# Retention scores in alternating halves, and two thirds of the feed-forward transposes by VectorE and DMA, in a two-block transformer

## The chip, the cores and the metric

The kernel runs on one core of one Trainium2 chip. The metric is the device time of one execution in microseconds (us).

## What is computed

Two blocks, one after the other, on a sequence of 256 rows of width 1024. The first block has two layers: retention with memory attention, a feed-forward, differential attention with memory attention, a feed-forward. The second has one layer: a state-space mixer beside a forgetting attention, and a feed-forward whose 5632 columns go through a causal convolution of three taps along the sequence. What the change touches is this:

```python
# retention, per head (dk 64): scores, decayed by distance
s_in = jnp.einsum('bnihd,bnjhd->bnhij', q, k) * d_in
# first block, both layers (FFN_DIM 2816)
gu = h @ w_gate_up[layer]
x = x + (jax.nn.silu(gu[..., :FFN_DIM]) * gu[..., FFN_DIM:]) @ w_down[layer]
# second block (D_FF 2816, three taps)
h = causal_depthwise_conv(x @ w_up, conv_w, conv_b)
gate, val = jnp.split(h, 2, axis=-1)
x = x + (jax.nn.silu(gate) * val) @ w_down
```

## The kernel before

All large products are computed in three matmuls of a rounded type: each operand is a high part and a low part, and high x high, high x low and low x high are summed in PSUM. Weights come by DMA in units of 256 rows by up to 512 columns (512 KB) into a ring of four staging buffers (`st`); ACT casts a unit to its high part (`wh`), DVE subtracts to get the low part (`wl`), each in a ring of six buffers. Activations stand with the sequence (256 rows, two tiles `t` of 128) in the partitions after a projection, and have to be turned before they can be the left operand of the next product: TensorE transposes blocks of 128x128 into PSUM, and ACT and DVE split the result into `lth` and `ltl` (ring of ten).

**Feed-forward.** `ffn` walks over six chunks of columns, five of 512 and one of 256. For a chunk, `act` runs a gate projection and a value (up) projection, each eight steps of the inner dimension by two `t` by three matmuls: 48 slots. The order is act(0), act(1), down(0), act(2), down(1), act(3) and so on, where down(n) adds the product of chunk n with `w_down` (four units, which all stay in their buffers until both `t` are done) into four PSUM banks of the pool `psa`, which has five. So what turns a chunk has one down section and the next chunk's two projections in which to finish, and for chunk 0 the projections alone.

In `ffn1` (first and second feed-forward) ACT writes the activated gate to `sg`, DVE multiplies it with the value projection, and a task per `t` transposes four blocks and splits them (lines 777 to 787). In `ffn2` (third) ACT copies each projection to `uu`; `conv_tiles` (line 823) transposes half a chunk at a time into one bank, in the order channel block by `t`, so that a channel's 256 positions stand in one partition; `conv` computes the taps out of PSUM into `cc`; then gate and value are multiplied and split.

**Retention.** `pair_task` in `mixer0` (line 974) computes for two heads, which lie in partitions 0 to 63 and 64 to 127 of `qkT`, the scores of both sequence tiles in one PSUM bank per head: two matmuls for the first head, its multiplication with the decay on DVE, then the same for the second.

**Order.** The program is written by a planner (`Weave`) that keeps an estimated clock per engine. Side work is a task (a generator) that says when it can go on; `poll` is called between the matmuls and emits the steps whose planned time has come, and `fill` emits weight DMAs, casts and subtractions when buffers come free. Every engine then runs its instructions in the order in which they were emitted. All DMAs are issued from the queue of SyncE (SP), line 257. All operations go through one helper and carry line 89.

Of the kernel before, what the change touches and what calls it, by code (L numbers as in the profile page):

```python
# [7 lines left out]
F32 = mybir.dt.float32  # L8
# [214 lines left out]
def _build(tc, a, out, stop):  # L223
# [6 lines left out]

    cp, wp, lp, nrm, sm = pool("cp"), pool("wp"), pool("lp"), pool("nrm"), pool("sm")
    ps_pools = pool("psm", space=PSUM), pool("psa", space=PSUM)


    def ring(p, n, tag, bufs, dtype=F32):
# [29 lines left out]

    W.clock["Q"] = 500.0

    def rsqrt(ss, n, inv):

        v, y = small([P, n], "r"), small([P, n], "r")  # L270
        G.tensor_scalar(v, ss, inv, EPS, op0=ALU.mult, op1=ALU.add)
        G.tensor_tensor(y, v, mhalf[:, :n], op=ALU.pow)
        return y
# [16 lines left out]
    def transposes(ps, srcs):  # L290
        for i, s_ in enumerate(srcs):
            T.transpose(ps[:, i * P : (i + 1) * P], s_, ident)

    def blocks(t_, n=4):
        return [t_[:, b * P : (b + 1) * P] for b in range(n)]
# [471 lines left out]
    def ffn1(l, H, nxt):  # L767
        with tc.tile_pool(name=W.name("ff"), bufs=1) as fp:
            w = a["w_gate_up"][l]
            sgr = ring(fp, 512, "sg", 6)  # L770

            def act(c0, nn, serial):
                sg = [sgr.get(True) for _ in range(2)]
                proj(w, H, c0, nn, lambda t, ps, r: S.activation(sg[t][:, :nn], ps[:, :nn], AF.Silu, scale=r), serial)
                got = [None, None]

                def task(t):
                    yield psa, 1
                    ps = psa.get(True)
                    transposes(ps, blocks(sg[t], nn // P))  # L780
                    sgr.close(sg[t])
                    yield
                    lt = yield from lt_tiles()
                    yield from split(lt[0][:, :nn], lt[1][:, :nn], ps[:, :nn])
                    psa.close(ps)
                    yield
                    return lt

                def ev(t, ps, r):
                    V.scalar_tensor_tensor(sg[t][:, :nn], ps[:, :nn], r, sg[t][:, :nn], op0=ALU.mult, op1=ALU.mult)  # L790
                    got[t] = go(task(t), W.clock["V"])

                proj(w, H, FF + c0, nn, ev)

                def both():
                    yield got
                    lts = [g.val for g in got]
                    return lambda k, t: tuple(z[:, (k * P - c0) : (k * P - c0) + P] for z in lts[t]), lts

                return go(both())  # L800

            return ffn(a["w_down"][l], H, nxt, act)
# [11 lines left out]
    def ffn2(H, nxt):  # L814
        with tc.tile_pool(name="ff2", bufs=1) as fp:
            w = a["w_up_2"]
            uur, ccr = ring(fp, 512, "uu", 6), ring(fp, 512, "cc", 6)

            def tiles(c0, nn, serial):
                us = [uur.get(True) for _ in range(2)]  # L820
                return us, proj(w, H, c0, nn, lambda t, ps, r: S.activation(us[t][:, :nn], ps[:, :nn], AF.Copy, scale=r), serial)

            def conv_tiles(us, c0, q):
                yield psa, 1
                ps = psa.get(True)
                transposes(ps, [us[t][:, (2 * q + b) * P : (2 * q + b + 1) * P] for b in range(2) for t in range(2)])
                yield ccr, 1
                res = ccr.get(True)
                ch = c0 // P + 2 * q
                yield from conv(ps, [res[:, b * 256 : (b + 1) * 256] for b in range(2)], C_FW + 3 * ch, C_FB + ch, 3)  # L830
                psa.close(ps)
                yield
                return res

            def act(c0, nn, serial):
                ug, got_g = tiles(c0, nn, serial)

                def gate():
                    yield [got_g]
                    gts = []  # L840
                    for q in range(nn // 256):
                        gt = yield from conv_tiles(ug, c0, q)
                        gts.append(gt)
                    uur.close(*ug)
                    for gt in gts:
                        S.activation(gt[:], gt[:], AF.Silu)
                    yield
                    return gts

                gt_ = go(gate())  # L850
                uv, got_v = tiles(FF + c0, nn, False)

                def task():
                    yield [got_v, gt_]
                    lts = []
                    for q in range(nn // 256):
                        gt = gt_.val[q]
                        vt = yield from conv_tiles(uv, FF + c0, q)
                        V.tensor_tensor(gt[:], gt[:], vt[:], op=ALU.mult)
                        ccr.close(vt)  # L860
                        yield
                        lt = yield from lt_tiles()
                        yield from split(lt[0][:], lt[1][:], gt[:])
                        ccr.close(gt)
                        lts.append(lt)
                    uur.close(*uv)
                    yield

                    def lhs(k, t):
                        i = k - c0 // P  # L870
                        o = (i % 2) * 256 + t * P
                        return tuple(z[:, o : o + P] for z in lts[i // 2])

                    return lhs, lts

                return go(task())

            return ffn(a["w_down_2"], H, nxt, act)
# [51 lines left out]
    def mixer0(H, nxt, first):  # L930
# [43 lines left out]
        def pair_task(pair, deps):  # L974
            yield deps
            sTs = []
            for hh in range(2):
                yield psa, 1
                r0 = 64 * hh
                st = psa.get(True)  # L980
                T.matmul(st[:, 0:256], qkT[r0 : r0 + 64, 3 + pair, 0:P], qkT[r0 : r0 + 64, pair, :], start=True, stop=True)
                T.matmul(st[:, 256:384], qkT[r0 : r0 + 64, 3 + pair, P : 2 * P], qkT[r0 : r0 + 64, pair, P : 2 * P],
                         start=True, stop=True)
                yield sTr, 1
                sT = sTr.get(True)
                V.tensor_tensor(sT[:], st[:, :384], dtab[:, 2 * pair + hh, :], op=ALU.mult)
                psa.close(st)
                sTs.append(sT)
            yield psa, 1
            ob = psa.get(True)  # L990
            for hh in range(2):
                sT = sTs[hh]
                v = [blk(768 + (2 * pair + hh) * P, t) for t in range(2)]
                T.matmul(ob[:, hh * P : (hh + 1) * P], sT[:, 0:P], v[0], start=True, stop=True)
                o1 = ob[:, 256 + hh * P : 256 + (hh + 1) * P]
                T.matmul(o1, sT[:, P : 2 * P], v[0], start=True, stop=False)
                T.matmul(o1, sT[:, 2 * P : 3 * P], v[1], start=False, stop=True)
                sTr.close(sT)
            yield
            on = onr.get(True)  # L1000
            yield from head_norm(ob, hsq, on)
            c, r = divmod(1536 + pair * 256, 512)
            while c not in E:
                yield 500
            yield [E[c]]
            for t in range(2):
                V.tensor_tensor(on[:, t * 256 : (t + 1) * 256], on[:, t * 256 : (t + 1) * 256],
                                u[c, t][:, r : r + 256], op=ALU.mult)
            yield psa, 1
            ps = psa.get(True)  # L1010
            transposes(ps, blocks(on))
            onr.close(on)
            yield
            lt = yield from lt_tiles()
# [796 lines left out]
```

## Time and profile before

| | us |
|---|---|
| median of 3 runs | 1037.08 (1036.85 to 1037.44) |
| the profiled execution | 1037.33 |
| its span, first to last instruction | 1035.4 |
| TensorE busy | 1027.5 |
| VectorE busy | 672.8 |
| ScalarE busy | 603.8 |

Busy times and rows are of the one profiled execution. Matmuls overlap in the pipeline, so a row's duration is longer than the slot between two starts; what a TensorE instruction costs is read from starts. The three feed-forwards lie at about 136 to 321, 428 to 614 and 842 to 1036 us.

### The profile page before, as it was taken

The numbers are of one execution on the slowest core, as the hardware profiler recorded it, in microseconds if no ns is written. First come the engines' busy times: TensorE is split into PE (matmuls) and PEld (weight loads), VectorE is DVE, ScalarE is ACT, GpSimd is POOL, SyncE is SP. The second block draws the span as 40 slices with busy tenths as digits, with TensorE's granted clock in tenths as the row PEclk, the third lists the DMA queues.
The fourth block names the chain that finished last, engine by engine and source line by source line (L and its number), as shares of the span: only waits on it lengthen the run. The fifth ranks groups of instructions, "written<-read, shape, count | busy, mean of one in ns | idle before, by whom it ended". The sixth has DMA issues, their size and how long they took to land.

```text
span 1035.4 us, 14058 instructions
## 1 busy us (share of the span) xinstructions
PE 1027.5 (99%) x5177; PEld 856.5 (83%) x5177; DVE 672.8 (65%) x1013; ACT 603.8 (58%) x974; POOL 68.1 (7%) x93
## 2 busy tenths in 40 slices
PE   9999999999999999999999999999999999999998
PEld 7878888888898778888888988888888888888887
DVE  5665575554556887755454467878888577767755
ACT  7647564444445886644444446686776566656553
POOL 1121000000001231100000001100300010000000
PEclk9999999999999999999999999999999999999999
DMA  7763555655565433565565457515523655566533
GB/s 248 261 203 127 163 185 181 192 182 155 182 203 171 142 122 124 182 210 190 151 204 192 150 151 220 186 41 179 167 82 99 193 161 178 171 196 204 177 116 114
DMA packets 98822, 174.93 MB, mean 169 GB/s; under 512 B 6976, under 2 KB 22080, under 8 KB 98624
## 3 DMA queue, kind: packets, MB, share of 16 engines
q1 hardware_dynamic: 98752, 174.02, 53.3%
q8 instruction: 41, 0.67, 0.3%
q14 instruction: 29, 0.24, 0.1%
HBM read 172.95 MB, written 1.05 MB: 168 GB/s over the span
## 4 chain that ended last, share of the span: by engine, by line
PE 92%; ACT 2%; DVE 2%; DMA 2%; POOL 1%; issue 1%; SPq 0%; ACTq 0%
PE psm L89 59%; PE psa L89 33%; DMA st<-w_in 1%; POOL s8r L89 1%; DMA xt<-x 1%; ACT wh L89 1%; ACT pd L89 0%; DVE wl L89 0%; POOL s16r L89 0%; DVE s L89 0%; SPq L257 0%; DVE pd L89 0%; ACT qkT L89 0%; POOL s4r L89 0%; DVE s16g L89 0%
## 5 line engine op out<-in xcount | busy, mean ns | idle before, releaser
L89 DVE TENSOR_TENSOR wl<-st,wh 128x1024 fp32r<-128x1024 f32 (+2 forms) x339 | 389.9, 1169 | 212.3 <-ACT wh L89 211.4
L89 ACT CAST wh<-st 128x1024 fp32r<-128x1024 f32 (+2 forms) x339 | 334.8, 1007 | 228.0 <-PE psm L89 100.5
L89 PE MATMUL psm<-wh,lth 128*128 128x512 f32 (+2 forms) x1024 | 395.8, 387 | 0.0
L89 PE MATMUL psm<-wl,lth 128*128 128x512 f32 (+2 forms) x1024 | 385.8, 377 | 0.0
L89 PE MATMUL psm<-wh,ltl 128*128 128x512 f32 (+2 forms) x1024 | 381.1, 377 | 0.1
L89 PEld LDWEIGHTS psm<-wh,ltl 128*128 128x128 f32 x1024 | 192.6, 188 | 36.8 <-DVE ltl L89 0.8
L89 PEld LDWEIGHTS psm<-wh,lth 128*128 128x128 f32 x1024 | 192.9, 188 | 33.7 <-issue 1.2
L89 PEld LDWEIGHTS psm<-wl,lth 128*128 128x128 f32 x1024 | 193.0, 188 | 32.9 <-DVE wl L89 1.0
L89 PE MATMUL psa<-wh,lth 128*128 128x512 f32 x328 | 132.2, 403 | 0.0
L89 PE MATMUL psa<-wl,lth 128*128 128x512 f32 x328 | 128.0, 390 | 0.0
L89 PE MATMUL psa<-wh,ltl 128*128 128x512 f32 x328 | 105.1, 390 | 0.0
L89 PEld LDWEIGHTS psa<-wh,ltl 128*128 128x128 f32 x328 | 61.6, 188 | 13.2
L89 PEld LDWEIGHTS psa<-wh,lth 128*128 128x128 f32 x328 | 61.7, 188 | 11.2
L89 PEld LDWEIGHTS psa<-wl,lth 128*128 128x128 f32 x328 | 61.7, 188 | 11.2
L89 DVE SCALAR_TENSOR_TENSOR cc<-psa,ccol,cc 128x255 f32<-128x255 f32 (+1 forms) x88 | 36.3, 476 | 18.5 <-ACT cc L89 18.3
L89 POOL TENSOR_SCALAR s1n<-s1n 128x1 f32<-128x1 f32 x14 | 5.1, 368 | 469.6 <-ACT sq L89 469.5
L89 DVE SCALAR_TENSOR_TENSOR sg<-psm,s1n,sg 128x512 f32<-128x512 f32 (+1 forms) x24 | 17.0, 707 | 20.6 <-PE psm L89 20.5
L89 ACT ACTIVATE cc<-psa,ccol 128x256 f32<-128x256 f32 x44 | 22.4, 560 | 12.9 <-PE psa L89 12.6
L89 ACT CAST lth<-psa 128x512 fp32r<-128x512 f32 (+1 forms) x30 | 16.6, 555 | 22.4 <-PE psa L89 22.3
L89 ACT ACTIVATE sq<-xt 128x512 f32<-128x512 f32 x24 | 15.3, 636 | 21.5 <-DVE xt L89 20.9
L89 DVE TENSOR_TENSOR ltl<-psa,lth 128x512 fp32r<-128x512 f32 (+1 forms) x30 | 19.6, 653 | 12.7 <-ACT lth L89 12.7
L89 ACT ACTIVATE sg<-psm,s1n 128x512 f32<-128x512 f32 (+1 forms) x24 | 15.7, 653 | 14.4 <-PE psm L89 14.4
(210 smaller groups left out, 856.3 us busy)
## 6 DMA issues: line engine op xcount, KB each, us to landing
st<-w_gate_up SPq DMA_DIRECT2D x80, 512.0 KB, 4.3
st<-w_in SPq DMA_DIRECT2D x67, 512.0 KB, 4.3
st<-w_down SPq DMA_DIRECT2D x66, 512.0 KB, 4.7
st<-w_up SPq DMA_DIRECT2D x40, 512.0 KB, 3.8
st<-w_out SPq DMA_DIRECT2D x32, 512.0 KB, 3.8
st<-w_in SPq DMA_DIRECT2D x30, 256.0 KB, 3.9
st<-w_mem_kv SPq DMA_DIRECT2D x8, 512.0 KB, 4.9
st<-w_gate_up SPq DMA_DIRECT2D x16, 256.0 KB, 2.8
```

The source lines that it names most:

```text
L89: f(*args, **kw)
```

## The change

A helper `flip` turns two tiles of 128x512 without TensorE. DVE transposes every square of 32x32 (two instructions into `sq32`, 128x1024); four DMAs write the result to a buffer in memory, one for each quarter of the partitions, in runs of 128 elements (512 B); one DMA reads the buffer back into `fl` (128x1024), in which the columns of a block lie in the order of an interleave. `unmix` and `mixed` are access patterns that undo it. All five DMAs are issued by SP.

In `ffn1` chunks whose first column is below 2048 (four of six) use it for both `t` together, and the splits read `fl`. In `ffn2` the same chunks use it once for the gate and once for the value; an ACT copy (`na`) puts the result in the order that `conv_tiles` takes, and the convolution reads `na` in SBUF in place of a PSUM bank. In `pair_task` two banks are taken at once, and the four score matmuls alternate between the heads.

```diff
+    scr = Ring(W, pool("scr", space=bass.MemoryType.DRAM), [2 * P, 512], F32, "scr", 4)
...
+    def flip(srcs, sqs, dst):
+        yield sqs, 1
+        sq = sqs.get(True)
+        for t, src in enumerate(srcs):
+            V.transpose(sq[:, t * 512 : (t + 1) * 512].rearrange("p (s b j) -> p s b j", s=4, b=4),
+                        src.rearrange("p (b s j) -> p s b j", b=4, s=4))
+        yield
+        m = scr.get(True)
+        m4 = m[:].rearrange("(t s i) (q n) -> q i (t s) n", t=2, s=4, q=4)
+        yield 300 + move(m[:], sq[:], [(m4[q], sq[32 * q : 32 * q + 32, :].rearrange("p (u n) -> p u n", u=8)) for q in range(4)])
+        sqs.close(sq)
+        yield 300 + move(dst[:], m[:], [(dst[:].rearrange("p (t n) -> p t n", t=2), m[:].rearrange("(t p) n -> p t n", t=2))])
+        scr.close(m)
...
+            sgr, sqs, flr = ring(fp, 512, "sg", 6), ring(fp, 1024, "sq32", 2), ring(fp, 1024, "fl", 2)
...
+                    yield from flip([z[:] for z in sg], sqs, fl)
+                    sgr.close(*sg)
+                    for t in range(2):
+                        lt = yield from lt_tiles()
+                        yield from split(mixed(lt[0][:]), mixed(lt[1][:]), unmix(fl, t))
...
-                    got[t] = go(task(t), W.clock["V"])
+                    if c0 >= 2048:
+                        got[t] = go(task(t), W.clock["V"])
+                    elif t == 1:
+                        got[:] = [go(flips(), W.clock["V"])]
...
+            def turned(us):
+                yield flr, 1
+                fl = flr.get(True)
+                yield from flip([z[:] for z in us], sqs, fl)
+                uur.close(*us)
+                yield nar, 1
+                na = nar.get(True)
+                S.copy(na[:].rearrange("p b (m j) -> p b m j", m=8), fl[:].rearrange("p (m b j) -> p b m j", m=8, b=4))
...
-                yield from conv(ps, [res[:, b * 256 : (b + 1) * 256] for b in range(2)], C_FW + 3 * ch, C_FB + ch, 3)
+                yield from conv(src, [res[:, b * 256 : (b + 1) * 256] for b in range(2)], C_FW + 3 * ch, C_FB + ch, 3)
...
-            for hh in range(2):
-                yield psa, 1
-                r0 = 64 * hh
-                st = psa.get(True)
-                T.matmul(st[:, 0:256], qkT[r0 : r0 + 64, 3 + pair, 0:P], qkT[r0 : r0 + 64, pair, :], start=True, stop=True)
-                T.matmul(st[:, 256:384], qkT[r0 : r0 + 64, 3 + pair, P : 2 * P], qkT[r0 : r0 + 64, pair, P : 2 * P],
-                         start=True, stop=True)
+            yield psa, 2
+            sts = [psa.get(True), psa.get(True)]
+            for b, cols in ((0, slice(0, 256)), (1, slice(256, 384))):
+                for hh, st in enumerate(sts):
+                    rows = slice(64 * hh, 64 * hh + 64)
+                    T.matmul(st[:, cols], qkT[rows, 3 + pair, b * P : (b + 1) * P], qkT[rows, pair, b * P :],
+                             start=True, stop=True)
+            for hh, st in enumerate(sts):
                 yield sTr, 1
```

## Rows read from the trace of the kernel before

**Rows 1.** The page, part 1: busy us, share of span, instructions.
```profile
PE 1027.5 (99%) x5177; PEld 856.5 (83%) x5177; DVE 672.8 (65%) x1013; ACT 603.8 (58%) x974; POOL 68.1 (7%) x93
```
**Rows 2.** Chain of waits in time, first feed-forward: start us, us, what.
```profile
191.03 21.76 PE psm L89 x96
212.79 11.80 PE psa L89 x56
```
**Rows 3.** Stretches, one chunk each: us, busy per engine, clock, DMA share, GB/s.
```profile
212.79:246.35 33.56, 33.56 (x155) 27.81 (x153) 17.14 (x16) 14.77 (x16) 0.00 (x0) 1.00 0.62 187
921.70:956.17 34.47, 34.47 (x161) 28.57 (x161) 23.23 (x32) 20.68 (x29) 0.00 (x0) 1.00 0.61 184
```
**Rows 4.** Groups by form, TensorE: transposes; busy, mean ns, idle before.
```profile
L89 PE MATMUL psa<-pcol,sg 128*128 128x128 f32 x88 | 13.5, 271 | 0.0
L89 PE MATMUL psa<-pcol,uu 128*128 128x128 f32 x88 | 13.2, 272 | 0.0
```
**Rows 5.** TensorE in order of time: four transposes in the first feed-forward.
```profile
178.84 0.39 PE L89 MATMUL psm<-wh,ltl 128*128 128x512 f32 x1
179.07 0.60 PE L89 MATMUL psa<-pcol,sg 128*128 128x128 f32 x4
...
179.98 0.39 PE L89 MATMUL psa<-wh,lth 128*128 128x512 f32 x1
```
**Rows 6.** TensorE in order of time, mixer0: one head's scores, then two.
```profile
36.39 0.39 PE L89 MATMUL psm<-wh,ltl 128*128 128x512 f32 x1
36.71 0.92 PE L89 MATMUL psa<-qkT 64*128 64x256 f32 x4
...
38.12 0.40 PE L89 MATMUL psm<-wh,ltl 128*128 128x512 f32 x1
...
49.76 0.39 PE L89 MATMUL psm<-wh,ltl 128*128 128x512 f32 x1
50.08 1.57 PE L89 MATMUL psa<-qkT 64*128 64x256 f32 x8
...
52.15 0.40 PE L89 MATMUL psm<-wh,ltl 128*128 128x512 f32 x1
```
**Rows 7.** TensorE in order of time, mixer1: two halves' scores, alternating.
```profile
346.34 0.39 PE L89 MATMUL psm<-wh,ltl 128*128 128x512 f32 x1
346.66 0.93 PE L89 MATMUL psa<-qkT 64*128 64x128 f32 x8
...
348.08 0.39 PE L89 MATMUL psm<-wh,ltl 128*128 128x512 f32 x1
```
**Rows 8.** Groups by form, ACT and DVE.
```profile
L89 ACT CAST wh<-st 128x1024 fp32r<-128x1024 f32 x305 | 314.4, 1050 | 196.0 <-PE psm L89 88.9 <-PE psa L89 54.6 <-DMA st<-w_down 12.2
L89 ACT CAST lth<-psa 128x512 fp32r<-128x512 f32 x26 | 15.2, 583 | 22.3 <-PE psa L89 22.3
L89 ACT CAST lth<-cc 128x512 fp32r<-128x512 f32 x11 | 6.8, 619 | 15.0 <-DVE cc L89 14.9
L89 DVE TENSOR_TENSOR ltl<-psa,lth 128x512 fp32r<-128x512 f32 x26 | 17.9, 689 | 11.9 <-ACT lth L89 11.9
```
**Rows 9.** Instructions on tile st, SP's issues: ns min/median/max, first and last start.
```profile
L257 SPq DMA_DIRECT2D st<-w_gate_up x96: 367/368/702, 108.6 to 583.4; - x96
```
**Rows 10.** SP's waits, third feed-forward: us in total, times, longest.
```profile
SPq L257 <- DVE wl L89: 128.7, 57, 8.7
```
**Rows 11.** Stretch of a down section, instructions on st alone: DVE, ACT, clock, DMA.
```profile
921.70:933.50 11.80, 2.44 (x2) 3.33 (x4) 1.00 0.41 131
```
**Rows 12.** DMA issues: count, KB each, median us to landing.
```profile
st<-w_gate_up SPq DMA_DIRECT2D x80, 512.0 KB, 4.3
out<-xt SPq DMA_DIRECT2D x4, 256.0 KB, 2.2
```
**Rows 13.** TensorE in order of time, third feed-forward: a value's two half tiles.
```profile
864.82 0.60 PE L89 MATMUL psa<-pcol,uu 128*128 128x128 f32 x4
...
872.08 0.60 PE L89 MATMUL psa<-pcol,uu 128*128 128x128 f32 x4
```

More of the change, by code (lines that the diff above doesn't have):

```diff
@@ L266, in _build, with move @@
     W.clock["Q"] = 500.0
+    def move(dst, src, parts):
+        for d, s_ in parts:
+            nc.sync.dma_start(d, s_)
+        k, n = dst.tensor.name, src.size() if callable(src.size) else src.size
+        W.clock["Q"] = max(W.clock["Q"], W.now, W.done.get(src.tensor.name, 0.0)) + 480 * len(parts)
+        W.clock["D"] = max(W.clock["D"], W.clock["Q"] + 1100) + n * 4 / 360.0
+        W.done[k] = W.used[k] = W.clock["D"] + 900
+        W.used[src.tensor.name] = W.clock["D"]
+        W.by[k] = "D"
+        return W.done[k] - W.now
     def rsqrt(ss, n, inv):
@@ L292, in transposes, with unmix, mixed @@
             T.transpose(ps[:, i * P : (i + 1) * P], s_, ident)
+    def flip(srcs, sqs, dst):
[11 more added lines that the diff above has]
+        scr.close(m)
+    def unmix(dst, t):
+        return dst[:, t * 512 : (t + 1) * 512].rearrange("p (q b j) -> p b q j", q=4, b=4)
+    def mixed(ap):
+        return ap.rearrange("p (b q j) -> p b q j", q=4, b=4)
     def blocks(t_, n=4):
@@ L769, in ffn1 @@
             w = a["w_gate_up"][l]
-            sgr = ring(fp, 512, "sg", 6)
+            sgr, sqs, flr = ring(fp, 512, "sg", 6), ring(fp, 1024, "sq32", 2), ring(fp, 1024, "fl", 2)
             def act(c0, nn, serial):
@@ L787, in task, with flips @@
                     return lt
+                def flips():
+                    yield flr, 1
+                    fl = flr.get(True)
+                    yield from flip([z[:] for z in sg], sqs, fl)
+                    sgr.close(*sg)
+                    lts = []
+                    for t in range(2):
+                        lt = yield from lt_tiles()
+                        yield from split(mixed(lt[0][:]), mixed(lt[1][:]), unmix(fl, t))
+                        lts.append(lt)
+                    flr.close(fl)
+                    yield
+                    return lts
                 def ev(t, ps, r):
                     V.scalar_tensor_tensor(sg[t][:, :nn], ps[:, :nn], r, sg[t][:, :nn], op0=ALU.mult, op1=ALU.mult)
-                    got[t] = go(task(t), W.clock["V"])
+                    if c0 >= 2048:
+                        got[t] = go(task(t), W.clock["V"])
+                    elif t == 1:
+                        got[:] = [go(flips(), W.clock["V"])]
                 proj(w, H, FF + c0, nn, ev)
@@ L796, in both @@
                     yield got
-                    lts = [g.val for g in got]
+                    lts = got[0].val if len(got) == 1 else [g.val for g in got]
                     return lambda k, t: tuple(z[:, (k * P - c0) : (k * P - c0) + P] for z in lts[t]), lts
@@ L817, in ffn2 @@
             uur, ccr = ring(fp, 512, "uu", 6), ring(fp, 512, "cc", 6)
+            sqs, flr, nar = ring(fp, 1024, "sq32", 2), ring(fp, 1024, "fl", 2), ring(fp, (4, 256), "na", 2)
             def tiles(c0, nn, serial):
@@ L821, in tiles, with conv_tiles @@
                 return us, proj(w, H, c0, nn, lambda t, ps, r: S.activation(us[t][:, :nn], ps[:, :nn], AF.Copy, scale=r), serial)
-            def conv_tiles(us, c0, q):
-                yield psa, 1
-                ps = psa.get(True)
-                transposes(ps, [us[t][:, (2 * q + b) * P : (2 * q + b + 1) * P] for b in range(2) for t in range(2)])
+            def turned(us):
+                yield flr, 1
+                fl = flr.get(True)
+                yield from flip([z[:] for z in us], sqs, fl)
[3 more added lines that the diff above has]
+                S.copy(na[:].rearrange("p b (m j) -> p b m j", m=8), fl[:].rearrange("p (m b j) -> p b m j", m=8, b=4))
+                flr.close(fl)
+                yield
+                return na
+            def conv_tiles(us, c0, q, na):
+                if na is None:
+                    yield psa, 1
+                    ps = psa.get(True)
+                    transposes(ps, [us[t][:, (2 * q + b) * P : (2 * q + b + 1) * P] for b in range(2) for t in range(2)])
+                src = ps[:] if na is None else na[:, 2 * q : 2 * q + 2, :].rearrange("p b n -> p (b n)")
                 yield ccr, 1
@@ L829, in conv_tiles @@
                 ch = c0 // P + 2 * q
-                yield from conv(ps, [res[:, b * 256 : (b + 1) * 256] for b in range(2)], C_FW + 3 * ch, C_FB + ch, 3)
-                psa.close(ps)
+                yield from conv(src, [res[:, b * 256 : (b + 1) * 256] for b in range(2)], C_FW + 3 * ch, C_FB + ch, 3)
+                if na is None:
+                    psa.close(ps)
+                elif 2 * q + 2 == 4:
+                    nar.close(na)
                 yield
@@ L840, in gate @@
                     gts = []
+                    na = (yield from turned(ug)) if c0 < 2048 else None
                     for q in range(nn // 256):
-                        gt = yield from conv_tiles(ug, c0, q)
+                        gt = yield from conv_tiles(ug, c0, q, na)
                         gts.append(gt)
-                    uur.close(*ug)
+                    if na is None:
+                        uur.close(*ug)
                     for gt in gts:
@@ L853, in task @@
                 def task():
-                    yield [got_v, gt_]
+                    yield [got_v]
+                    na = (yield from turned(uv)) if c0 < 2048 else None
+                    yield [gt_]
                     lts = []
@@ L857, in task @@
                         gt = gt_.val[q]
-                        vt = yield from conv_tiles(uv, FF + c0, q)
+                        vt = yield from conv_tiles(uv, FF + c0, q, na)
                         V.tensor_tensor(gt[:], gt[:], vt[:], op=ALU.mult)
@@ L865, in task @@
                         lts.append(lt)
-                    uur.close(*uv)
+                    if na is None:
+                        uur.close(*uv)
                     yield
@@ L976, in pair_task @@
             sTs = []
-            for hh in range(2):
-                yield psa, 1
-                r0 = 64 * hh
-                st = psa.get(True)
-                T.matmul(st[:, 0:256], qkT[r0 : r0 + 64, 3 + pair, 0:P], qkT[r0 : r0 + 64, pair, :], start=True, stop=True)
-                T.matmul(st[:, 256:384], qkT[r0 : r0 + 64, 3 + pair, P : 2 * P], qkT[r0 : r0 + 64, pair, P : 2 * P],
-                         start=True, stop=True)
+            yield psa, 2
[6 more added lines that the diff above has]
+            for hh, st in enumerate(sts):
                 yield sTr, 1
```

## Prediction

> **What bounds the kernel now.** The page's busy times come first: TensorE (PE) is busy for 1027.5 of 1035.4 us, VectorE (DVE) for 672.8, ScalarE (ACT) for 603.8 [rows 1]. A full PE row says little by itself, so the second view is the chain of waits in order of time. Inside the feed-forwards it is nothing but PE: 96 matmuls in 21.76 us for the two projections of a chunk, then 56 instructions in 11.80 us for a down section [rows 2]. So a matmul of 512 columns has a slot of 21.76/96 = 0.2267 us, and no wait lies between them. An edit there is worth the PE slots that it removes, as long as weights and left operands still arrive in time. The third view is the table of stretches: in a steady chunk of the first feed-forward DVE works 17.1 of 33.6 us, ACT 14.8 and the DMA engines 62%; in the third DVE works 23.2 of 34.5, ACT 20.7, DMA 61% [rows 3].
>
> **Transposes removed.** A chunk below column 2048 (four of six) loses its TensorE transposes: two groups of four in each of the first two feed-forwards, four groups in the third. That is 64 of the 88 of sg and 64 of the 88 of uu [rows 4], 32 groups in all. One group: from the matmul before it (178.84) to the third matmul after it (179.98) [rows 5] are 1.14 us, where three slots take 0.68; it costs 0.46. The chain says the same: 11.80 less 48 slots of 0.2267 (10.88) is 0.92 for two groups [rows 2]. The gain is 32 x 0.46 = **14.7 us**, all of it on the path.
>
> **Scores in turns.** Retention's score matmuls use 64 rows of the array. Now two of a head stand together, then two of the other head on the other rows. Such a group of four records takes 38.12 - 36.39 = 1.73 us less 0.68 of ordinary slots, 1.05; where both heads stood in one row (eight records, head after head) 52.15 - 49.76 - 0.68 = 1.71 [rows 6]. Mixer1's heads hold the same shapes, already alternated between the halves: eight records in 348.08 - 346.34 - 0.68 = 1.06 [rows 7]. Before there are four single groups and one double one: 4 x 1.05 + 1.71 = 5.9; after, three alternated: 3.2. The gain is **2.7 us**, and nothing if the halves don't overlap here; I take 2.7, since rows 7 are the same shapes. The first wait for two free banks instead of one; the waiting is the program's planner's, behind which matmuls of the projections go on, and I cost it at nothing (if two banks are late, PE loses up to one group, 1 us).
>
> **What is added.** There are 16 round trips: four in each of the first two feed-forwards, eight in the third. Each has two DVE transposes of 128x512, four DMAs of 128 KB into memory in rows of 512 B (1024 packets), and one of 512 KB back. DVE: no row shows its square transpose; the ops of that size, 689 ns [rows 8], are the nearest, and twice that is the other end, for the four-way access pattern. In the third feed-forward a chunk has four: 23.2 + 4 x 0.69 = 26 us, at most 28.7, of the 32.6 us that a chunk has left (34.47 less 1.83). DVE becomes the bound only from 2.4 us for one. ACT gets a copy of 1024 columns per round trip in the third alone, 1.05 us like a weight cast [rows 8]: 20.7 + 2.1 of 32.6. Reading the conversions' sources from SBUF instead of PSUM I take at about the same price: a cast of 512 columns takes 583 ns from PSUM and 619 from SBUF [rows 8]. All of it lies beside PE.
>
> SP: a weight DMA costs its queue 0.37 us [rows 9], so five cost 1.8 us per round trip. In order on that queue the read-back waits until the write has landed, and weight loads stand behind it. They can wait: SP already waits for DVE to free staging, 128.7 us of the third feed-forward [rows 10], so loads run ahead with four staged units. Converted weights run ahead less: six buffers, of which a down section holds four, so two units of 2.72 us (12 matmuls), 5.4 us of cover. In such a section DVE converts only two, 2.44 us [rows 11].
>
> DMA engines: a chunk's 12 units of 256 packets take 0.62 x 33.56 us x 16 engines / 3072 = 108 ns for one packet of 2 KB. A packet of 512 B costs between a quarter of it (27 ns) and the whole (108), so the writes of a round trip take 1.7 to 6.9 us and the read 1.7. The first two feed-forwards reach at most 20.8 + 8.6 = 29.4 of 32.6 us, covered. The third has 21.0 + 6.9 = 28 at the low end and 38 at the high one. I take a value near the low end (bytes, not packets, as the load of 4.3 us for 512 KB beside 2.2 us for a 256 KB store suggests [rows 12]); the high end is a rival.
> The Trainium skill, page "DMA: Bandwidth & Descriptors", section Specifications, gives 512 B as the smallest transfer at line rate; by it the write costs the low end, an estimate of 1.7 us, and the sum stays as it is. No row here shows such a store.
>
> **The new wait.** After a projection ends: evacuation 0.7 us, transposes 1.4, one weight conversion ahead of them 1.2 [rows 11], four issues 1.5 [rows 9], landing 2.2 to 4.3 (I take 4), read-back 0.4 + 4.3 [rows 12], for a total of 13.5. The first two feed-forwards add a multiplication (0.7) and four splitting ops (some 2.7): 17 us. The third adds the copy with its queue (2): 15.5, then the convolution of one half tile, which today is paced 872.08 - 864.82 = 7.3 us [rows 13], some 6 without TensorE: halves at 21.5 and 27.5 us. These are wanted after the next chunk's projections and one down section (32.6 us), so they are in time, except for chunk 0, which has no down section between: 21.8 us and, for the second half, 24.5. That makes no wait in the first two feed-forwards and about **3 us** in the third (bounds 0 and 6).
>
> **Sum.** 1037.33 (this execution's own time; span 1035.4) - 14.7 - 2.7 + 3.0 = 1022.9. The median of the runs is 0.25 lower: **1022.7**.
>
> **Rivals.** (1) As forecast, 1019.5 to 1026: 62%. (2) The scores gain nothing: 1025.4, 8%. For it, the second group could sit where PE then waits for DVE; against it, rows 7. (3) Round trips land late everywhere: ACT and DVE are in order, so a copy that waits for the read-back holds up weight casts behind it. If both landings double, ACT stands 8 us instead of being covered for 5.4, and PE loses 2.6 us at perhaps four of the 16, 10 us: 1033, 16%, spread over 1026 to 1035. (4) **Slower:** packets bind, not bytes. In the third feed-forward a chunk has 21.0 + 2 x (1.7 + 64 p) us of DMA, with p the packet's time. From p = 64 ns DMA outlasts PE; from 98 ns four chunks give back all 17.4; at 108 ns each is 38.3 long, 5.6 over, 22.6 in all: 1037.3 - 17.4 + 22.6 = 1042.5. 9%: against it speaks that every other store and load here scales with its bytes. (5) The store is slower by an order, since its strides do part of the transposing: if each row of 512 B cost four packets of 108 ns, it would take 27.6 us and a round trip 29.3. The first feed-forwards' chunks would be 50.1 us long and the third's 79.6, 8 x 17.5 + 4 x 47.0 = 328 us: 1348, 2%. Against it, the innermost step of the copy is one element, and DVE has turned the squares before it.
> The Trainium skill, page "VectorE: DVE Perf Modes", section "The three transpose paths", warns of this: a plain copy whose strides do the transposing is 19 times slower than the transposing DMA when the innermost destination stride is large, and its rules give full 128x128 blocks to TensorE. By that factor on 1.7 us, an estimate of 32 us, the time would be near that of (5). (6) Effects cancel within 0.2% (2.1 us, what a measurement of this kernel can tell from no change): 3%.
> Together: faster 0.86, same 0.03, slower 0.11. The range takes (1), (2) and most of (3), with planner noise of 1 us below: 1018.8 to 1031.
>
> **What would show it.** Right: no sg transposes by TensorE but 24, chunks of 32.65 us in all three feed-forwards, a PE gap of some 3 us ahead of the third's first down section and none elsewhere; eight-record score groups of 0.85 us in mixer0; DVE transposes near 0.69 us. Wrong: PE waiting for wl or wh in the chunks (3), DMA share at 0.9 and more with loads landing far above 4.3 us (4, 5), a granted clock below 1.00 after the gap.

## The result and the profile after

The changed kernel takes 1019.81 us in the median (1019.48 to 1021.1, four runs); the kernel before, run beside it, 1037.26 (1036.85 to 1037.97, four runs). The ratio is 0.9833, 95% interval 0.9819 to 0.9847. The forecast was 1022.7: right in direction, the time inside the range and 2.9 us shorter than forecast. The profiled execution took 1019.89, with a span of 1018.1 us, 17.3 less than that of [rows 1]. One execution of a variant below took 3612 us, and its time and trace are left out.

The page of the changed kernel: busy us, share of the span, instructions; below it the two kinds of DMA of a round trip (count, KB each, median us to landing).

```profile
PE 1008.9 (99%) x5049; PEld 842.0 (83%) x5049; DVE 691.0 (68%) x1045; ACT 611.6 (60%) x982; POOL 67.8 (7%) x93
...
scr<-sq SPq DMA_DIRECT2D x64, 128.0 KB, 4.5
fl<-scr SPq DMA_DIRECT2D x16, 512.0 KB, 5.1
```

TensorE executes 128 instructions fewer, which are the 32 groups of four transposes, and is still busy 99% of the span: what was taken off its queue shortened the span. The chain of waits of the changed kernel shows the same chunk as [rows 2], then the third feed-forward (start us, us, what):

```profile
186.62 21.76 PE psm L89 x96
208.38 10.88 PE psa L89 x48
...
877.93 7.82 PE psa L89 x33
885.75 21.76 PE psm L89 x96
907.50 10.88 PE psa L89 x48
```

A down section of 11.80 us has become 10.88 us, its 48 matmuls and nothing else, in the first feed-forward and in the third. The stretches (columns as in [rows 3]): a steady chunk of the third, one of the first, and then the projections of the third's chunk 1, which alone cover the turning of chunk 0's value:

```profile
907.50:940.14 32.64, 32.64 (x146) 27.03 (x145) 25.76 (x37) 22.65 (x30) 0.00 (x0) 1.00 0.77 240
219.26:251.90 32.64, 32.64 (x145) 27.04 (x145) 18.24 (x19) 14.63 (x17) 0.00 (x0) 1.00 0.71 226
851.91:873.67 21.76, 21.76 (x97) 18.02 (x96) 17.77 (x29) 18.24 (x25) 0.00 (x0) 1.00 0.83 270
```

Both steady chunks last 32.64 us, where [rows 3] had 33.56 and 34.47. DVE is busy for 79% of the first row, 56% of the second and 82% of the third (17.77 of 21.76). Some 4 us behind that last stretch stands the only new wait of TensorE in a feed-forward. TensorE, VectorE and one row of ACT, in order of time:

```profile
877.93 0.50 PE L89 MATMUL psa<-wl,lth 128*128 128x512 f32 x1 [0.70 <-DVE wl L89]
```
```profile
874.08 1.30 DVE L89 STREAM_TRANSPOSE sq<-uu 128x512 f32<-128x512 f32 x2
876.05 0.69 DVE L89 TENSOR_TENSOR ltl<-cc,lth 128x512 fp32r<-128x512 f32 x1 [0.66 <-ACT lth L89]
876.65 3.49 DVE L89 TENSOR_TENSOR wl<-st,wh 128x1024 fp32r<-128x1024 f32 x3
```
```profile
874.46 1.04 ACT L89 CAST wh<-st 128x1024 fp32r<-128x1024 f32 x1
```

The low part of a `w_down` unit stood on VectorE behind `ltl`, and `ltl` waited 0.66 us for ACT, whose conversion `lth` began only at 875.40, behind a weight cast (874.46). The two squares of the next gate (874.08) had ended by then, so they didn't make this wait. PE stood 0.70 us. By starts, the down section takes 885.75 - 873.67 = 12.08 us instead of 10.88: the wait costs 1.2 us in all. By stage, the span's difference of 17.3 us is: mixer0 3.1 gained, the first feed-forward 3.7, the second 3.7, mixer2 0.7, the third feed-forward 6.3, the end behind TensorE's last instruction 0.3, less a start that was 0.5 later in this execution.

### The profile page after: what moved, and what is told of

It reads as the page before. It is cut to its first block, busy times and chain, and to the rows that moved or that the text cites. A ratio compares the mean times of both kernels' runs of the same rounds, so it can differ in the third digit from the quotient of the medians.

```text
span 1018.1 us, 13938 instructions
## 1 busy us (share of the span) xinstructions
PE 1008.9 (99%) x5049; PEld 842.0 (83%) x5049; DVE 691.0 (68%) x1045; ACT 611.6 (60%) x982; POOL 67.8 (7%) x93
## 4 chain that ended last, share of the span: by engine, by line
PE 93%; DVE 2%; ACT 2%; POOL 1%; DMA 1%; issue 1%; SPq 0%; ACTq 0%
PE psm L89 61%; PE psa L89 32%; POOL s8r L89 1%; DVE wl L89 0%; ACT pd L89 0%; DMA st<-w_in 0%; DMA fl<-scr 0%; DVE ltl L89 0%; ACT wh L89 0%; POOL s16r L89 0%; DVE s L89 0%; ACT lth L89 0%; DVE pd L89 0%; ACT qkT L89 0%; POOL s4r L89 0%
## 5 line engine op out<-in xcount | busy, mean ns | idle before, releaser
L89 DVE SCALAR_TENSOR_TENSOR cc<-na,ccol,cc 128x255 f32<-128x255 f32 (+1 forms) x64 | 27.2, 480 | 6.1 <-ACT cc L89 6.0
L89 ACT ACTIVATE uu<-psm,s1n 128x512 f32<-128x512 f32 (+1 forms) x24 | 15.6, 651 | 15.7 <-PE psm L89 15.6
L89 POOL TENSOR_TENSOR s16r<-s16r,mhalf 128x16 f32<-128x16 f32 x7 | 22.2, 3178 | 0.6
```

The source lines that it names most:

```text
L89: f(*args, **kw)
```

## Experiments

**The scores alone.** The kernel before with the diff of `pair_task` only:

```diff
-            for hh in range(2):
-                yield psa, 1
+            yield psa, 2
+            sts = [psa.get(True), psa.get(True)]
+            for b, cols in ((0, slice(0, 256)), (1, slice(256, 384))):
+                for hh, st in enumerate(sts):
```

> Only the score matmuls alternate; all feed-forward transposes stay on TensorE. Theory (the halves of the array overlap, and TensorE is the path in mixer0): 2.7 us less by the prediction's groups, 3.1 if pairs 1 and 2 stand together in one row as in the changed kernel, so a ratio of 0.9970 to 0.9974. Rival (the freed slots are filled by a later wait, such as that for the memory keys): no change, 1.000.

Measured: 1034.38 us (5 runs) against 1038.0, ratio 0.9964 (0.9951 to 0.9978). The stretch of mixer0 that holds all score groups, from the same matmul to the same matmul, in the kernel before and then in this one:

```profile
22.70:74.42 51.72, 51.20 (x253) 41.54 (x253) 35.32 (x45) 28.21 (x42) 10.96 (x14) 1.00 0.70 231
```
```profile
24.47:73.07 48.60, 48.08 (x253) 39.87 (x253) 35.09 (x45) 27.93 (x42) 10.72 (x14) 1.00 0.75 246
```

The same 253 instructions take 51.72 - 48.60 = 3.1 us less: the part is worth the same without the rest of the change. Another 0.5 of the 3.6 us lies in mixer2, which no part of the change touches (its account stands further below).

**The first two feed-forwards alone.** Scores and third feed-forward as before: in `ffn2` no chunk is turned by squares.

```diff
-                    na = (yield from turned(ug)) if c0 < 2048 else None
+                    na = (yield from turned(ug)) if c0 < 0 else None
```

(and the same for `uv`.)

> Only the first two feed-forwards use the round trip; scores and the third as before. Theory (slots alone, all added work covered): 16 groups of 0.46 us, 7.4 us less, chunks of 32.64 us and no TensorE wait in either feed-forward; ratio 0.9929. Rival (round trips late, weight casts held up): TensorE waits in the chunks, less than 5 us gained.

Measured: 1029.55 us (4 runs), ratio 0.9918 (0.9905 to 0.9932). The kernel before, run beside it, took 1038.0, so 8.5 us are gained where sixteen groups at 0.46 are 7.4. In the trace the two feed-forwards are 3.7 us shorter each, as the theory has it; the other 1.1 us lie outside them, 0.75 of it in mixer2. No wait of TensorE is new in these two, and a chunk's two pieces of the chain are 21.76 and 10.88 us, as in the changed kernel.

**The third feed-forward alone.** Scores as before, in `ffn1` all chunks by TensorE:

```diff
-                    if c0 >= 2048:
+                    if c0 >= 0:
```

> Only the third feed-forward uses the round trip; scores and the first two as before. Theory: 16 groups, 7.4 us less, minus the wait at chunk 0's down section, which is 0.7 us in the changed kernel's trace: 6.7 us less, ratio 0.9935. The prediction's 3 us of waiting: 4.4 less, 0.9958. Rival (packets bind): DMA share near 1 and nothing gained, 1.000.

Measured: 1030.74 us (4 runs), ratio 0.9932 (0.9919 to 0.9946): 7.4 gained and 0.7 to 1.2 paid would be 1030.6 to 1031.1. The wait stands at the same place, ahead of the same 33 matmuls, so it belongs to this feed-forward and not to what precedes it:

```profile
887.10 1.22 DVE wl L89
...
888.36 7.78 PE psa L89 x33
```

**The third without chunk 0.** Chunk 0 of the third, the only one without a down section as cover, goes back to TensorE; all else as changed.

```diff
-                    na = (yield from turned(ug)) if c0 < 2048 else None
+                    na = (yield from turned(ug)) if 0 < c0 < 2048 else None
```

> As the changed kernel, but chunk 0 of the third feed-forward stays on TensorE. Theory (the only wait of the change is at chunk 0's down section, 0.7 us, because chunk 0 has no down section as cover): 4 groups come back, 1.84 us, and the wait of 0.7 us is gone: 1.1 us above the changed kernel's 1019.8, so 1020.9, with no TensorE wait in the third feed-forward. Rival (the wait moves to the next chunk that is turned): 1021.7.

Measured: 1021.31 us (4 runs), ratio 0.9848 (0.9831 to 0.9864), 1.5 more than the changed kernel, where four groups given back less the wait are 1.84 less 0.7 to 1.2. The times (1020.7 to 1023.4) don't tell the theory's 1020.9 from the rival's 1021.7; the trace does. TensorE waits nowhere in the third: the chain is PE from the projections straight into the down section.

```profile
862.94 13.62 PE psm L89 x60
876.56 10.88 PE psa L89 x48
```

So the wait is chunk 0's own; it doesn't move to chunk 1.

**The store twice.** To test whether packets or bytes limit the DMA engines, each round trip writes a second copy of 512 KB, which nothing reads:

```diff
+        m = scr2.get(True)
+        m4 = m[:].rearrange("(t s i) (q n) -> q i (t s) n", t=2, s=4, q=4)
+        move(m[:], sq[:], [(m4[q], sq[32 * q : 32 * q + 32, :].rearrange("p (u n) -> p u n", u=8)) for q in range(4)])
```

> As the changed kernel, but every round trip stores its 512 KB twice, first to a second buffer that nobody reads: twice the small packets, four more issues, a later read-back, nothing more on DVE or ACT. Theory (latency counts only where there is no cover): the chain grows by some 3.5 us, the second half of chunk 0 in the third feed-forward is 4 us late, the first two feed-forwards have 4 us of slack there and lose nothing: 1019.8 + 4 = 1024, and steady chunks stay at 32.64 us. Rival (packets bind the third feed-forward): steady chunks longer than 32.64 us and DMA share at 0.95 or more, over 1030.

Measured: 1029.23 us (4 runs), ratio 0.9923 (0.9908 to 0.9937): 9.4 slower than the changed kernel, more than expected. But a steady chunk is as long as without the second store; the first row below is one. The second is two microseconds behind a wait in chunk 0's down section, and the third is the largest wait of TensorE's weight loads in the third feed-forward.

```profile
894.19:926.83 32.64, 32.64 (x146) 27.03 (x145) 20.94 (x27) 18.54 (x23) 0.00 (x0) 1.00 0.89 274
```
```profile
878.00:880.00 2.00, 2.00 (x6) 1.58 (x7) 2.00 (x4) 0.41 (x1) 0.00 (x0) 0.55 1.11 348
```
```profile
PEld psa L89 <- ACT lth L89: 6.6, 2, 3.6
```

The two stores that such a chunk adds raise the DMA share from 0.77 to 0.89 of 32.64 us, with about the same loads in both stretches (3292 and 3328 packets of 2 KB): 0.12 x 32.64 / 2 = 1.96 us each, or 1.96 x 16 / 1024 = 31 ns for a packet of 512 B. Counted one by one in the two traces, these packets take 27 ns in the median and 33 and 30 on average. That is near the end of the bounds that counts bytes (27 ns), far from the one that counts packets (108). At a share of 0.89 the chunk still ends on TensorE. Nearly all of the loss lies at chunk 0, where the share was 0.83 already and is now 1.04 of the 21.76 us: the packets' times add up to more than the 16 engines have, and a read-back stood for 8.4 us in the chain of waits:

```profile
872.49 8.39 DMA fl<-scr
```

The second store also holds SP's queue longer (eight issues take 4.8 us, four 2.2); this and the fuller DMA engines were not told apart. Behind the two waits, of 3.2 and 2.3 us, some matmuls run at 0.43 us instead of 0.227, in the stretch shown at a granted clock of 0.55, most of it at the lower level of 1.2 GHz. Behind the second wait 32 matmuls take 9.16 us, where 32 slots of 0.2267 are 7.25: the clock costs another 1.9 us.

**Squares three times.** VectorE's work tripled where the trip begins: every transpose is executed three times into the same tile ahead of the store.

```diff
-        for t, src in enumerate(srcs):
+        for t, src in [(t, s_) for t, s_ in enumerate(srcs) for _ in range(3)]:
```

> As the changed kernel, but every DVE transpose of squares is run three times in place: 2.6 us of DVE more per round trip, nothing more in memory traffic. Theory (DVE is covered up to the length of a chunk): steady chunks of the third feed-forward rise from 26 to 31 us of DVE and stay at 32.64 us; only chunk 0 waits, by 2.6 us more: 1022.5. Rival (weight casts behind the transposes on DVE's queue come late everywhere): TensorE waits for wl in the steady chunks too, 1026 or more.

Measured: 1037.3 us (10 runs), ratio 0.9996 (0.9986 to 1.0006): the whole gain is gone, and the theory on record with it. A transpose stays at 703 ns, so a tile costs 2.1 us, under the 2.4 from which the prediction called DVE the bound. The first two feed-forwards lose 0.2 us each. Of the 16.0 us by which the span is longer than the changed kernel's, the third's chunk 0 loses 11.1; its down section, and the waits of TensorE's weight loads there:

```profile
873.00:889.33 16.33, 7.58 (x20) 4.85 (x20) 16.11 (x30) 10.24 (x17) 0.00 (x0) 0.69 0.91 287
```
```profile
PEld psa L89 <- ACT lth L89: 9.6, 2, 8.1
```

DVE is busy for 16.11 of 16.33 us while TensorE is for 7.58. Another 4.8 us go in a steady chunk, in the down section of chunk 2: there TensorE waits for a weight's low part that stands on VectorE behind the six squares of the next value (VectorE, then TensorE):

```profile
952.12 4.28 DVE L89 STREAM_TRANSPOSE sq<-uu 128x512 f32<-128x512 f32 x6
```
```profile
957.56 0.50 PE L89 MATMUL psa<-wl,lth 128*128 128x512 f32 x1 [2.87 <-DVE wl L89]
```

The granted clock falls to 0.50 there too, from 959.0 to 962.4. So the rival's wait for `wl` in a steady chunk came as well, once, although VectorE was busy for only 27.42 of the 32.65 us before that section. For chunk 0 two causes remain: DVE's load, or each store's later start (four squares, 2.8 us).

**The extra squares behind the store.** The same load, without the later start: the four extra transposes go to a spare tile, after the four DMAs have been issued.

```diff
+        for src in [s_ for s_ in srcs for _ in range(2)]:
+            z = sqs.spare.get(True)
+            V.transpose(z[:].rearrange("p (s b j) -> p s b j", s=4, b=4), src.rearrange("p (b s j) -> p s b j", b=4, s=4))
```

> The four extra square transposes of each round trip now stand behind the issue of the store, into a spare tile: VectorE's work is that of the kernel with every transpose three times, the chain from a projection to its left operand is not lengthened by 2.8 us at its head. Theory (VectorE's load in the third feed-forward's first chunk makes the loss, since conversions of weights queue behind the extra squares): 1030 us or more, with TensorE waits for wl and lth in that chunk as before. Rival (the loss came from the later store): 1020 to 1023 us, waits of some 1 us as in the changed kernel.

Measured: 1030.15 to 1031.8 us in three executions, 1030.35 in the median, ratio 0.9936 (0.9919 to 0.9953). The rival's 1020 to 1023 is excluded: some 10.5 of the 17.5 us come from the load alone, and some 7 more when the store starts later as well. The same kernel once more, for its trace:

> The same kernel as with the extra squares behind the store, for its trace. Its times were 1030.2 to 1031.8, so VectorE's load makes most of the loss. Theory: in the third feed-forward's first chunk VectorE is busy for over 93% of some 16 us, as with the extra squares ahead of the store, and TensorE waits there for conversions (wl, lth), some 5 to 8 us, with a lower granted clock behind it. Rival: the loss is spread over the chunks, a little in each, and the first chunk holds under 3 us.

Measured: 1029.65 us (1 run), span 1027.9, 9.8 above the changed kernel's, and all of it in chunk 0 of the third: up to there the stages of both traces agree within 0.1 us, behind a start that is 0.4 earlier, and the down section that started at 907.50 starts at 917.27. So the rival, a loss spread over the chunks, is excluded. The projections that had DVE at 82%, the down section behind them, a steady chunk, and TensorE's waits:

```profile
851.91:873.67 21.76, 21.76 (x97) 17.78 (x96) 19.42 (x31) 16.17 (x23) 0.00 (x0) 1.00 0.74 237
873.00:889.33 16.33, 8.39 (x24) 5.45 (x24) 15.80 (x28) 10.91 (x17) 0.00 (x0) 0.69 0.69 219
895.51:928.15 32.64, 32.64 (x146) 27.04 (x145) 28.64 (x40) 20.42 (x26) 0.00 (x0) 1.00 0.82 258
```
```profile
PE psa L89 <- ACT lth L89: 5.5, 1, 5.5
PE psa L89 <- DVE wl L89: 2.5, 1, 2.5
```

DVE is at 89% in the first row and at 97% in the second (15.80 of 16.33), and TensorE stands 7.9 us there, as the theory has it; the granted clock of 0.69 adds the rest. In a steady chunk DVE is at 88% and nothing waits. So it isn't the share alone; the likely reason is that a steady chunk has a down section more in which a late operand can still arrive. The chain through chunk 0 runs over VectorE, in the order of its queue, and at its end over a read-back (the chain, then VectorE in order of time):

```profile
871.66 1.15 DVE wl L89
872.82 0.39 SPq L258
...
873.39 6.02 DMA fl<-scr
879.42 1.05 ACT na L89
```
```profile
877.21 2.94 DVE L89 STREAM_TRANSPOSE spare<-uu 128x512 f32<-128x512 f32 x4
880.07 0.65 DVE L89 TENSOR_TENSOR cc<-cc,cc 128x512 f32<-128x512 f32 x1
```

The larger part is VectorE's own order: the product from which ACT makes the late `lth` stood behind four extra squares of the next gate and ended at 880.7. ACT's queue adds 0.8 us: `lth` began at 881.5, behind the copy `na` of that gate, which had waited for the read-back. This read-back was issued 0.9 us later than in the changed kernel (872.49) and took 6.02 us where it took 4.18 there. In SP's queue it stands behind a weight load (`SPq L258`) that waits for DVE to free its staging buffer (`wl`): a late DVE also delays a transfer that it has nothing to do with.

**Five chunks.** The fifth chunk (of 512 columns as well) by squares too, in all three feed-forwards: 2048 becomes 2560 in three lines.

> As the changed kernel, but with a fifth chunk (columns 2048 to 2559) by the round trip in all three feed-forwards. Theory (a slot saved counts while the chain ends in time): 8 groups more, 3.7 us below the changed kernel's 1019.8, so 1016.1; chunk 4 has a down section and a half-wide chunk ahead of its own down section, 22.4 us, where the chain in the third feed-forward was measured at 18.8 and 24.8 us for the two halves, wanted at 22.4 and 25.1, so a wait of at most 1 us: 1016 to 1017. Rival (the tail's trips come late, since loads, casts and splits pile up there): the gain is eaten, 1019 to 1022.

Measured: 1017.66 us (4 runs), ratio 0.9809 (0.9795 to 0.9824), faster than both kernels, and between the theory's 1016 to 1017 and the rival's 1019 to 1022. The first two feed-forwards gain 0.92 and 0.93 more, two groups each. The third gains 0.3 of the 1.84 that its four groups are worth: in its last chunks TensorE's weight loads now wait, too:

```profile
PEld psa L89 <- DVE wl L89: 2.0, 3, 1.1
```

One wait of 1.1 is chunk 0's. The others stand behind the chunk of 256 columns, whose projections cover half of what those of a full chunk do.

**Five chunks in the first two only.**

```diff
-                    if c0 >= 2048:
+                    if c0 >= 2560:
```

> Five chunks by squares in the first two feed-forwards, four in the third. Theory (a chunk by squares gives back 0.92 us wherever a down section of another chunk covers it): 1019.8 - 4 x 0.46 = 1018.0, no new TensorE wait. Rival (the last chunk of 256 columns is too short a cover, as in the third): 1019 or more, with waits for lth ahead of the fifth chunk's down section.

Measured: 1017.93 us (4 runs), ratio 0.981 (0.9794 to 0.9827), as the theory has it (1018.0); the waits of TensorE's matmuls in the third are again a single one of 0.7 us. In `ffn1`, which has two squares per chunk instead of four and no convolution, even the short chunk covers the trip.

**Five, but only the gate in the third.** As the version with five chunks, with the fifth chunk's value by TensorE:

```diff
-                    na = (yield from turned(ug)) if c0 < 2048 else None
+                    na = (yield from turned(ug)) if c0 < 2560 else None
```

(and `c0 >= 2560` in `ffn1`; the line of `uv` stays.)

> In the first two feed-forwards the fifth chunk goes by squares too, in the third only the fifth chunk's gate does; its value stays with TensorE. Four transposing groups fewer in the first two, two fewer in the third than in the changed kernel. Theory (the tail waits of the version with five chunks come from the late value of the fifth chunk): 1019.8 - 4 x 0.46 - 2 x 0.46 = 1017.0, no TensorE wait in the tail. Rival (any trip of the fifth chunk makes VectorE late in the tail): 1017.7 or more, with the same waits of some 3 us.

Measured: 1023.02 us (4 runs), ratio 0.9857 (0.984 to 0.9873), 3.2 above the changed kernel: the theory falls, and the rival's 1017.7 or more holds with another wait than the one it named. TensorE in the tail, and the first microseconds behind:

```profile
998.71 1.09 PE L89 MATMUL psa<-pcol,uu 128*128 128x128 f32 x4 [3.33 <-DVE cc L89]
```
```profile
999.00:1001.00 2.00, 2.00 (x8) 1.71 (x7) 1.54 (x3) 1.16 (x3) 0.00 (x0) 0.50 0.00 0
```

A group of transposes stands in TensorE's queue and needs a `psa` bank that the convolution of the group before it reads; that group stood at 994.78, and its convolution started on DVE only at 996.91, behind ACT's evacuation, an activation and the first tap. The bank came free 3.33 us late, and the granted clock was 0.50 up to 1001 and 0.55 in the microsecond after: 18.49 us for the last 76 instructions, where the changed kernel has 16.82. Together 5.0 us lost against 6 x 0.46 = 2.8 gained, 2.2 of the 3.2 measured. One of the four executions took 1020.54 us, with a granted clock of 1.00 on average where the others have 0.996 to 0.998, so it did not pay the clock's part. Here a TensorE group came into a tail where its bank is late; why the planner put it there, and whether mixing the two ways within a chunk does this in general, was not tried.

## Why the prediction was right, and where its terms were off

**Transposes removed.** Right, term and place: 0.46 us for a group from starts [rows 5] and from the chain [rows 2] gave 14.7 us. In their traces the first two feed-forwards alone gave what 16 groups are worth (7.35 of 7.36 us), and the third gave 6.3, with 1.2 gone to its wait.

**Scores.** Mis-sized: 2.7 forecast, 3.1 measured. The price of a switch was right. In the changed kernel pair 0 costs 38.67 - 36.92 - 0.68 = 1.07 us, mixer1's 1.06 [rows 7]. TensorE in order of time, pair 0, then pairs 1 and 2:

```profile
36.92 0.39 PE L89 MATMUL psm<-wh,ltl 128*128 128x512 f32 x1
37.24 0.92 PE L89 MATMUL psa<-qkT 64*128 64x256 f32 x8
...
38.67 0.40 PE L89 MATMUL psm<-wh,ltl 128*128 128x512 f32 x1
...
49.28 0.39 PE L89 MATMUL psm<-wh,ltl 128*128 128x512 f32 x1
49.60 1.58 PE L89 MATMUL psa<-qkT 64*128 64x256 f32 x16
...
51.68 0.40 PE L89 MATMUL psm<-wh,ltl 128*128 128x512 f32 x1
```

The prediction counted three groups, 3.2 us. The planner put pairs 1 and 2 in one row of 16 records, 51.68 - 49.28 - 0.68 = 1.72. So it is 1.07 + 1.72 = 2.8, and 5.9 - 2.8 = 3.1.

**The new wait.** Place right, size wrong: 3.0 forecast (bounds 0 and 6), 0.7 measured as TensorE's idle time and 1.2 by starts. What TensorE waited for was not the left operand, as forecast, but a weight's low part behind it on VectorE; a wait for `wl` stood among the prediction's signs of being wrong. The working is followed by the value trip of chunk 0 in the changed kernel, whose projection ends at 851.9 (VectorE, SP's queue and ACT in order of time):

```profile
851.62 0.70 DVE L89 STREAM_TRANSPOSE sq<-uu 128x512 f32<-128x512 f32 x1
852.83 0.71 DVE L89 STREAM_TRANSPOSE sq<-uu 128x512 f32<-128x512 f32 x1 [0.51 <-ACT uu L89]
```
```profile
853.57 2.05 SPq L272 DMA_DIRECT2D scr<-sq  x4
...
859.46 0.37 SPq L272 DMA_DIRECT2D fl<-scr  x1
```
```profile
863.83 1.04 ACT L89 COPY na<-fl 128x1024 f32<-128x1024 f32 x1
...
869.39 0.61 ACT L89 CAST lth<-cc 128x512 fp32r<-128x512 f32 x1
...
875.40 0.62 ACT L89 CAST lth<-cc 128x512 fp32r<-128x512 f32 x1
```

From the first issue to the read-back's issue are 5.9 us (5.5 estimated), from there to the copy 4.4 (4.7), from one half tile to the next 6.0 (6 estimated). What failed are two terms of overhead. The head, evacuation, transposes and a weight conversion, was summed to 3.3 us and took 853.57 - 851.9 = 1.7: the first tile's squares are under way while the second is still evacuated, and no conversion stood ahead. The copy "with its queue" was 2 and took 1.0, since ACT was free. Together 2.6 us, so that the halves come 2.7 us earlier than forecast, at 18.8 and 24.8 us for 21.5 and 27.5. They are just in time, and what is late instead is a weight's low part, which the queues of ACT and DVE put behind the second half.

**VectorE as cover.** Wrong in reason, though the number was not needed: a bound "only from 2.4 us for one" transpose came from a sum over a steady chunk. With the extra squares behind the store it holds there: nothing waits in such a chunk at 28.64 of 32.64 us. With the squares at 2.1 us a tile ahead of the store it doesn't: a steady down section lost 4.8 us, chunk 0, which has 21.8 us of cover for its value, lost 11.1, and the whole gain was gone. The step that failed is the sum of busy time over a steady chunk as a test of cover: it leaves out in which order VectorE's queue comes to an operand, and it has to be made where the cover is shortest. A square transpose itself costs what was taken as the nearest row, 0.69 us (groups by form of the changed kernel):

```profile
L89 DVE STREAM_TRANSPOSE sq<-uu 128x512 f32<-128x512 f32 x16 | 10.8, 697 | 4.9 <-ACT uu L89 4.9
L89 DVE STREAM_TRANSPOSE sq<-sg 128x512 f32<-128x512 f32 x16 | 10.4, 686 | 0.0
```

**DMA.** Right: 31 ns for a packet of 512 B, near the low end (27); rivals 4 and 5 fall with it. The argument from bytes was weaker than it reads: in the kernel before, `w_in` loads of 256 KB took 3.9 us and those of 512 KB 4.3; it is the packets that decide. The Trainium skill, page "DMA: Bandwidth & Descriptors", section Specifications, puts line rate at 512 B and more; the 31 ns, beside 27 for a quarter of a 2 KB packet, nearly agree. The Trainium skill, page "VectorE: DVE Perf Modes", section "The three transpose paths", warns of a factor of 19, against the transposing DMA, for a plain copy that transposes by its strides when the innermost destination stride is large. Here the copy's innermost run is 512 B long, and the read-back could be issued 5.9 us after the first of the four stores, so the warning didn't apply. Rival 3, late round trips everywhere, was refuted as it stands (one wait in 16 trips). Where a second store or more squares were put in, waits for late operands did appear, at chunk 0 and, with the squares ahead of the store, in one steady down section.

**What was not in the sum.** mixer2 is 0.7 us shorter, 0.45 of it in its first 26 us. There ACT waits 2.5 us for a `w_in` load in the kernel before (at 635.4) and 1.2 in the changed one (624.3), while TensorE, VectorE, ACT and SP execute the same instructions in the same order: it is the time at which a load lands, and not the planner's order. mixer2 is 0.5 to 0.75 us shorter in each of the first three experiments as well, so no one part of the change makes it; the kernel before has one trace, and whether other executions of it differ stays open. The wait's 1.8, mixer2's 0.7, the scores' 0.4, the end's 0.3 and 0.2 more from the transposes make 3.4; less the 0.5 by which the start was later, that is the 2.9 that the forecast was off.

## What to carry to other kernels

Where TensorE is the whole chain, an edit is worth the slots it removes, read from starts, and its new work is free as long as the shortest cover holds it. So the cover of off-path engines is to be summed first at the first and the last piece of a loop: here the steady chunks took twice the stores, and the extra squares behind the store, without a wait, and the first chunk of the third feed-forward took neither. And busy time alone doesn't settle it: with the extra squares ahead of the store a steady chunk waited too, at a VectorE share of 84%, because an operand stood behind them in the queue. How far to go with such a change is a matter of each loop: five chunks pay in the light feed-forwards (1017.9) and hardly in the heavy one (1017.7 with all three).

## What the runs showed of the hardware

A DVE transpose of 32x32 squares over 128x512 in a four-way access pattern takes 686 to 703 ns, about as much as a subtraction of that size (689) [rows 8]. Most surprising was the price that a wait has beyond itself: behind 3.3 us of standing TensorE ran for some microseconds at the lower clock level (0.50), with matmuls at 0.43 us, and lost 1.7 us more; 1.9 us were lost behind 2.3 us of standing with the store twice. Behind the changed kernel's 0.7 us the granted clock stayed at 1.00. The prediction's sign for that, a clock below 1.00 after the gap, therefore didn't appear.
